# Two branch gates by Strassen's algorithm in a hybrid attention layer, and its forgetting gates in two stages

## The chip, the cores and the metric

One of the eight cores of a Trainium2 chip runs the kernel. The metric is device microseconds of one execution. TensorE multiplies, VectorE (DVE), ScalarE (ACT) and GpSimd (POOL) do the elementwise work, SyncE (SP) issues most loads. The five engines run their own instruction queues in order and wait for each other on semaphores.

## The reference

A layer over 512 frames of 1024 channels, all in float32. With u the normalized input:

```python
proj = u @ w_in          # GLA q,k,v,out-gate g,low-rank alpha | FoX q,k,v,forget | memory query | 3 gates of 1024
y_gla = (rmsnorm(gla(q, k, v, log_a)) * silu(g)) @ w_gla_o      # 4 heads, chunks of 64 frames
y_fox = forgetting_attention(q, k, v, log_f) @ w_fox_o          # 8 heads, causal softmax
y_mem = memory_attention(q, mem) @ w_mem_o                      # 4 heads, 256 memory tokens
merged = sigmoid(gate_gla) * y_gla + sigmoid(gate_fox) * y_fox + sigmoid(gate_mem) * y_mem
h = x + merged @ w_out
h = h + square(relu(rmsnorm(h) @ w_ff1)) @ w_ff2
out = rmsnorm(h)
```

Each of the three gates is a product of 512 x 1024 by 1024 x 1024. A sigmoid is computed as half of 1 + tanh(x/2).

## The kernel before

Every large product runs in three passes. An operand is split into hi, its rounding to the fast float32 format, and lo, the rest; `mm3` (L150 to L153) then adds hi*hi, hi*lo and lo*hi in PSUM. A weight chunk of 128 x 1024 floats (512 KB) is loaded by SP into a ring of three raw buffers; `split_w` makes hi by a cast on ScalarE (L141) and lo by a difference on VectorE (L142), into rings of three hi and three lo tiles. So the split of one chunk can begin when the chunk three earlier has been used up. The activations' hi and lo (`uhi`, `ulo`) stay in SBUF for all projections. `split` (L203, L204) does the same for other operands.

A projected tile (`gT`) is 128 output channels by 512 frames: eight k-steps of `mm3`, 24 matmuls of 512 columns. A generator yields after each `mm3`; one such yield is called a unit here.

The order of TensorE's instructions is that of the program. The other engines' queues are ordered by a planner that simulates when each instruction would be ready. The attention stages are written as lists of steps (scores, transposes, values of one head), and `weave` puts units of other projections between the steps so that TensorE has work while the other engines do the softmax or the decays:

- FoX stage: eight heads, woven with 128 units: GLA keys and queries, the FoX query and key tiles of pairs 2 and 3 (`fox_pair`), GLA values (`gvg`, which takes four PSUM tiles at once) and the four output gates `gla_g`.
- Memory stage: four heads; its own query tiles are steps, and the forgetting branch (`branch("gate_fox", ...)`) is the fill: 96 units.
- GLA stage: `decays`, `key_turn`, `gla_scores`, `states`, `gla_values`, `gla_turn` over two pairs of heads, woven with the memory branch, 96 units.
- Then the GLA branch runs alone, and after it the output projection and the FFN.

A branch does, for each of eight tiles j: the gate tile, tanh on ScalarE (L629), the output tile (12 matmuls), the product (tanh + 1) * y on VectorE (L642, L644); for the second and third branch GpSimd adds it into `acc` (L645). The last branch also splits `acc` for the output projection.

The FFN already uses Strassen's algorithm. Its weight sums are made in DRAM by GpSimd's DMAs, 32 copies and accumulating copies in a fixed order. `next_sum` issues one with every second weight chunk; each waits for that chunk's cast, and for the sum that it builds on.

## Time and profile before

| | |
|---|---|
| median of 3 executions | 845.01 us (844.64 to 846.56) |
| the profiled execution | 845.09 us, span 843.3 us |
| mean granted TensorE clock | 0.995 |
| TensorE busy | 826.6 us (98%) |
| VectorE busy | 557.7 us (66%) |
| ScalarE busy | 438.9 us (52%) |
| GpSimd busy | 92.1 us (11%) |

The profile is of one execution. Busy time of matmuls overlaps, since they are pipelined, so the starts of two instructions give a truer price than the duration of one. In rows of a timeline the first number is the start in us, the second the duration in us, and a bracket holds the idle time of the engine before the instruction and what ended it. In rows of groups, the numbers behind the first bar are the busy time in us and the mean duration in ns, then the engine's idle time just before and its releasers.

### The profile page before, as it was taken

How to read it: one execution, taken by the hardware profiler on the slowest of the kernel's cores; microseconds unless marked ns; L12 is line 12 of the kernel's file. 1: busy time of each engine (PE TensorE's matmuls, PEld its weight loads, DVE VectorE, ACT ScalarE, POOL GpSimd, SP SyncE). 2: the span in 40 equal slices, each digit the busy share in tenths (PEclk: the TensorE clock that was granted, in tenths of full speed). 3: DMA queues.
4: the chain of work that ended last, by engine and by line, in shares of the span. 5: the costliest groups of instructions: out<-in, count | busy, mean ns of one | idle time of the engine just before them, and what ended most of it. 6: DMA issues, size and time to landing. Idle time of an engine off the chain costs nothing.

```text
span 843.3 us, 11909 instructions
## 1 busy us (share of the span) xinstructions
PE 826.6 (98%) x4553; PEld 709.9 (84%) x4553; DVE 557.7 (66%) x899; ACT 438.9 (52%) x695; POOL 92.1 (11%) x114
## 2 busy tenths in 40 slices
PE   8999999999999999999999999999999999999994
PEld 6888888888888888787888889998998899889983
DVE  5856767656444556574543457896689678878896
ACT  6765757654333341321332335875577367637763
POOL 1001000000000021222222100011001100100011
PEclk9999999999999999999999999999999999999998
DMA  8525545354556546257677632978767966895552
GB/s 312 192 100 198 153 151 167 110 174 132 171 147 171 179 137 188 48 174 229 200 181 212 208 123 70 291 173 198 243 196 165 219 218 175 193 256 186 142 97 102
DMA packets 36872, 147.16 MB, mean 174 GB/s; under 512 B 4624, under 2 KB 5584, under 8 KB 34768
## 3 DMA queue, kind: packets, MB, share of 16 engines
q1 hardware_dynamic: 28144, 96.06, 33.0%
q0 software_dynamic: 7168, 46.14, 26.0%
q10 hardware_dynamic: 1504, 4.21, 1.4%
q8 instruction: 35, 0.57, 0.3%
q14 instruction: 21, 0.17, 0.1%
HBM read 144.27 MB, written 31.49 MB: 208 GB/s over the span
## 4 chain that ended last, share of the span: by engine, by line
PE 92%; DVE 4%; DMA 1%; issue 1%; ACT 1%; POOL 0%; SPq 0%; POOLq 0%; DVEq 0%
PE mm L151 25%; PE mm L152 25%; PE mm L153 24%; PE a L152 3%; PE a L151 3%; PE a L153 3%; DVE h L959 1%; DVE lo L204 1%; PE a L794 1%; DMA xn<-in_xN_dram 1%; DMA raw<-in_wst_dram 1%; PE a L516 1%; PE a L811 1%; PE a L517 1%; PE a L549 1%
## 5 line engine op out<-in xcount | busy, mean ns | idle before, releaser
L142 DVE TENSOR_TENSOR wlo<-raw,whi 128x1024 fp32r<-128x1024 f32 x75 | 95.7, 1279 | 80.1 <-ACT whi L141 78.9
L141 ACT CAST whi<-raw 128x1024 fp32r<-128x1024 f32 x75 | 78.8, 1052 | 121.3 <-PE mm L152 96.0
L151 PE MATMUL mm<-uhi,whi 128*128 128x512 f32 x352 | 139.4, 396 | 0.0
L153 PE MATMUL mm<-uhi,wlo 128*128 128x512 f32 x352 | 137.3, 390 | 0.0
L152 PE MATMUL mm<-ulo,whi 128*128 128x512 f32 x352 | 137.2, 390 | 0.0
L203 ACT CAST hi<-raw 128x1024 fp32r<-128x1024 f32 x65 | 68.2, 1049 | 47.5 <-PE mm L152 34.4
L204 DVE TENSOR_TENSOR lo<-raw,hi 128x1024 fp32r<-128x1024 f32 x65 | 79.5, 1223 | 18.6 <-ACT hi L203 18.6
L153 PEld LDWEIGHTS mm<-uhi,wlo 128*128 128x128 f32 x352 | 66.1, 188 | 14.1
L151 PEld LDWEIGHTS mm<-uhi,whi 128*128 128x128 f32 x352 | 66.1, 188 | 13.5 <-issue 0.7
L152 PEld LDWEIGHTS mm<-ulo,whi 128*128 128x128 f32 x352 | 66.2, 188 | 12.7
L152 PE MATMUL mm<-lo,ch 128*128 128x512 f32 x160 | 62.5, 391 | 0.9 <-DVE lo L204 0.9
L152 PE MATMUL mm<-u2l,hi 128*128 128x256 f32 x224 | 63.4, 283 | 0.0
L153 PE MATMUL mm<-u2h,lo 128*128 128x256 f32 x224 | 63.4, 283 | 0.0
L151 PE MATMUL mm<-u2h,hi 128*128 128x256 f32 x224 | 63.4, 283 | 0.0
L203 ACT CAST hi<-b 128x1024 fp32r<-128x1024 f32 x40 | 41.9, 1048 | 40.9 <-PE mm L153 30.4
L153 PE MATMUL mm<-hi,cl 128*128 128x512 f32 x160 | 62.3, 389 | 0.0
L151 PE MATMUL mm<-hi,ch 128*128 128x512 f32 x160 | 62.3, 389 | 0.0
L204 DVE TENSOR_TENSOR lo<-b,hi 128x1024 fp32r<-128x1024 f32 x40 | 48.8, 1223 | 18.2 <-ACT hi L203 18.2
L1143 POOL DMA_DIRECT2D b<-in_wst_dram x32 | 27.6, 863 | 272.2 <-DVE lo L204 209.8
L151 PE MATMUL mm<-u2sh,hi 128*128 128x256 f32 x168 | 47.5, 283 | 0.0
L152 PE MATMUL mm<-u2sl,hi 128*128 128x256 f32 x168 | 47.5, 283 | 0.0
L153 PE MATMUL mm<-u2sh,lo 128*128 128x256 f32 x168 | 47.5, 283 | 0.0
(353 smaller groups left out, 1905.4 us busy)
## 6 DMA issues: line engine op xcount, KB each, us to landing
raw<-in_wst_dram SPq DMA_DIRECT2D x121, 512.0 KB
b<-in_wst_dram POOLq DMA_DIRECT2D x32, 512.0 KB, 5.5
raw<-T SPq DMA_DIRECT2D x28, 512.0 KB
T<-in_wst_dram POOLq DMA_DIRECT2D x12, 1024.0 KB, 8.5
b<-in_wst_dram SPq DMA_DIRECT2D x16, 512.0 KB
T<-in_wst_dram POOLq DMA_DIRECT2D x6, 512.0 KB, 5.3
nFb<-dF ACTq DMA_DIRECT2D x6, 512.0 KB
xn<-in_xN_dram SPq DMA_DIRECT2D x4, 512.0 KB
```

The lines of the kernel that those rows point to most:

```text
L141: cast = nc.scalar.copy(hi, raw)
L142: nc.vector.tensor_tensor(lo, raw, f(hi), op=ALU.subtract)
L151: nc.tensor.matmul(ps, lh, rh, start=start, stop=False)
L152: nc.tensor.matmul(ps, lh, rl, start=False, stop=False)
L153: nc.tensor.matmul(ps, ll, rh, start=False, stop=stop)
L203: nc.scalar.copy(hi, src)
L204: return nc.vector.tensor_tensor(lo, src, f(hi), op=ALU.subtract).ins
L516: nc.tensor.matmul(ps[:, :w], q, K[e][:, 0, :w], start=True, stop=False)
L517: nc.tensor.matmul(ps[:, :w], q, K[e][:, 1, :w], start=False, stop=True)
L549: nc.tensor.matmul(po[:, q0:], vv, PTl[:, c0:c0 + w], start=False, stop=n == 3)
L794: nc.tensor.matmul(ps[:, t, :], kk[:, sl], qq[:, sl], start=True, stop=True)
L1143: nc.gpsimd.dma_start(to[i], wst[index["B", q, i, x]], accum_op=ALU.add)
```

## The change

The gates of the memory and GLA branches are no longer computed tile by tile. Each gate is two groups of four tiles, and a group is one Strassen product of 2 x 2 blocks: weights in blocks 512 channels deep (11, 12, 21, 22; a new kind of chunk, "W"), frames in two halves of 256, seven products of 24 matmuls of 256 columns in place of four tiles of 24 matmuls of 512. All four groups come after the GLA stage (`gate_group`).

- The sums of weight blocks (`plus`) are four GpSimd additions of 128 x 1024 a group. Each is then split like any weight chunk.
- The sums of the activations' blocks are made once: `u_sum` forms two from `uhi` and `ulo` on GpSimd, placed in the GLA stage, and `gate_lefts` forms two more on VectorE and splits all four, in the first group.
- The products are combined on VectorE into `ct` tiles, where the tanh also runs. The output tiles of a group stand between the products.
- The GLA output gates `gla_g` move from the FoX stage to the GLA stage. The forgetting branch is divided: all eight output tiles and the first four gates stay in the memory stage (`fox_out`), the last four gates go to the GLA stage (`fox_late`), with `acc` kept in between.
- So the three attention stages have 96, 64 and 64 units of fill. `weave` takes a weight for each step; the memory stage's steps are in a new order, and the two empty steps of the GLA stage go.
- `next_sum` starts with chunk 19 instead of 9.
- The residual's loads are issued behind the last group, and buffers are shared: raw blocks lie in the tiles of the residual (even groups) or in a tile of the output projection and the `u_sum` tiles (odd groups).

```diff
@@ -45,11 +45,14 @@
     L += [("N", "w_in", 2 * j, OFF["gv"]) for j in range(4)]
     for n, c in (("gg", 4), ("mq", 4)):
         L += [("T", "w_in", OFF[n] + P * j) for j in range(c)]
-    for g, o in (("gate_fox", "w_fox_o"), ("gate_mem", "w_mem_o"), ("gate_gla", "w_gla_o")):
-        for j in range(KT):
-            L.append(("T", "w_in", OFF[g] + P * j))
-            if j % 2 == 0:
-                L.append(("O", o, j // 2))
+    for j in range(KT):
+        L.append(("T", "w_in", OFF["gate_fox"] + P * j))
+        if j % 2 == 0:
+            L.append(("O", "w_fox_o", j // 2))
+    for g, o in (("gate_mem", "w_mem_o"), ("gate_gla", "w_gla_o")):
+        for i in range(2):
+            L += [("W", g, i, b) for b in ("11", "12", "21", "22")]
+            L += [("O", o, 2 * i + 1), ("O", o, 2 * i)]
...
@@ -119,7 +122,7 @@
     def next_sum(after):
         chunk_n[0] += 1
-        op = next(sums, None) if chunk_n[0] > 8 and chunk_n[0] % 2 else None
+        op = next(sums, None) if chunk_n[0] > 18 and chunk_n[0] % 2 else None
-    def weave(steps, units, *gens):
+    def weave(steps, units, *gens, shares=None):
         fill = chain(*gens)
         done = 0
+        shares = shares or [1] * len(steps)
         for i, st in enumerate(steps):
             st()
-            due = units * (i + 1) // len(steps)
+            due = units * sum(shares[:i + 1]) // sum(shares)
             while done < due and next(fill, fill) is not fill:
                 done += 1
         run(fill)
...
-        def gla_g(j):
...
-        steps = []
+        steps, shares = [], []
         for h in range(1, 10):
-            for fn, i in ((fox_values, h - 2), (fox_turn, h - 1), (fox_scores, h)):
+            for fn, i, n in ((fox_values, h - 2, 3), (fox_turn, h - 1, 2), (fox_scores, h, 3)):
                 if 0 <= i < 8:
                     steps.append(partial(fn, i))
-        weave(steps, 128, gla_k(0), gla_k(1), gla_q(0), gla_q(1), fox_pair(2), fox_pair(3), gvg,
-              *[gla_g(j) for j in range(4)])
+                    shares.append(n)
+        weave(steps, 96, gla_k(0), gla_k(1), fox_pair(2), gla_q(0), gla_q(1), fox_pair(3), gvg, shares=shares)
...
-    def branch(gate, wo, oh, ol, n, last=None):
...
+    def o_tile(ow, j, oh, ol, ps):
+        for k in range(4):
+            mm3(ps, ow[0][:, j % 2, k, :], ow[1][:, j % 2, k, :], oh[k], ol[k], k == 0, k == 3)
+            yield
...
+    def fox_gate(j, evac):
+        def tanh(ps):
+            th = mp.tile([P, S], F32, tag="th", name=nm("th"))
+            nc.scalar.activation(th, ps, AF.Tanh, scale=0.5)
+            evac(th)
+        return gT(("T", "w_in", OFF["gate_fox"] + P * j), uhi, ulo, tanh)
+    def fox_out():
         cur = {}
         for j in range(KT):
+            if j < 4:
+                yield from fox_gate(j, lambda th: cur.update(th=th))
             if j % 2 == 0:
+                ow = get_o("w_fox_o", j)
             py = mmt()
+            for i, _ in enumerate(o_tile(ow, j, ofh, ofl, py)):
+                if i == 3:
+                    if j < 4:
+                        nc.vector.scalar_tensor_tensor(acc[j], cur["th"], 1.0, py, op0=ALU.add, op1=ALU.mult)
+                    else:
+                        nc.scalar.copy(acc[j], py)
+                yield
+    def fox_late():
+        for j in range(4, KT):
+            yield from fox_gate(j, lambda th: nc.vector.scalar_tensor_tensor(acc[j], th, 1.0, acc[j], op0=ALU.add, op1=ALU.mult))
...
+        Q, A, T, V_ = (lambda i: run(mem_q(i))), mem_scores, mem_turn, mem_values
+        steps = [(Q, 1), (A, 0), (Q, 2), (T, 0), (A, 1), (V_, 0), (Q, 3), (T, 1), (A, 2), (V_, 1), (T, 2), (A, 3), (V_, 2),
+                 (T, 3), (V_, 3)]
+        weave([partial(*st) for st in steps], 64, fox_out())
     kvst.close()
...
+        def gla_g(j):
...
+        def u_sum(n):
+            x = xsum[n] = xsp.tile([P, 4, 256], F32, tag=f"x{n}", name=f"x{n}")
+            (ah, al), (bh, bl) = (A21, A22) if n == 1 else (A11, A21)
+            nc.gpsimd.tensor_tensor(x, ah, bh, op=ALU.subtract)
+            nc.gpsimd.tensor_tensor(x, x, al, op=ALU.add)
+            nc.gpsimd.tensor_tensor(x, x, bl, op=ALU.subtract)
+        xsum = {}
+        A11, A12, A21, A22 = ([f(t[:, 4 * k:4 * k + 4, 256 * i:256 * i + 256]) for t in (uhi, ulo)] for i in range(2) for k in range(2))
+        steps = (
+            (decays, 0, 10), (key_turn, 0, 3), (gla_scores, 0, 3), (states, 0, 3), (gla_scores, 1, 3), (gla_values, 0, 3),
+            (gla_values, 1, 3), (decays, 1, 3), (gla_turn, 0, 4), (gla_turn, 1, 4), (key_turn, 1, 3), (gla_scores, 2, 3),
+            (states, 1, 3), (u_sum, 1, 0), (gla_scores, 3, 3), (gla_values, 2, 3), (gla_values, 3, 4), (u_sum, 3, 0), (gla_turn, 2, 3),
+            (gla_turn, 3, 3))
+        weave([partial(fn, i) for fn, i, _ in steps], 64, *[gla_g(j) for j in range(4)], fox_late(), shares=[n for *_, n in steps])
...
+        S1, S2, S4 = ([quad(own_tile(i, g)) for g in "hl"] for i in range(3))
+        S3 = [t[:, 0:4, 256:512] for t in (uhi, ulo)]
+        GATE = {1: [t[:, 0:4, 0:256] for t in (uhi, ulo)], 2: [t[:, 4:8, 0:256] for t in (uhi, ulo)],
+                4: [t[:, 4:8, 256:512] for t in (uhi, ulo)], 5: S1, 6: S2, 3: S4, 7: S3}
+        def gate_lefts():
+            split(*S1, xsum[1])
+            for to, (ah, al) in ((S2, A11), (S4, A12)):
+                nc.vector.tensor_tensor(xsum[1], ah, xsum[1], op=ALU.subtract)
+                nc.vector.tensor_tensor(xsum[1], xsum[1], al, op=ALU.add)
+                split(*to, xsum[1])
+            split(*S3, xsum[3])
+        def spare(odd, n):
+            if not odd:
+                return h_tile(n, "wb")
+            return own_tile(3, "hl"[n], F32) if n < 2 else xsp.tile([P, 1024], F32, tag=f"x{2 * n - 3}", name=nm("wb"))
+        def gate_group(gate, wo, oh, ol, i, odd, lefts=None, last=None):
+            raw = {"11": wp.tile([P, 1024], F32, tag="raw", name=nm("raw"))}
+            raw.update({b: spare(odd, n) for b, n in (("12", 0), ("21", 2), ("22", 3))})
+            total = spare(odd, 1)
+            X = [op_.tile([P, 2, S], F32, tag=f"ct{n}", name=nm("ct")) for n in range(2)]
+            (c11, c21), (c12, c22) = ([x[:, :, 256 * n:256 * n + 256] for n in range(2)] for x in X)
+            for b in ("11", "21", "12", "22"):
+                nc.sync.dma_start(raw[b], wst[index["W", gate, i, b]])
+            def plus(to, x, y):
+                nc.gpsimd.tensor_tensor(to, x, y, op=ALU.add)
+            def vec(to, x, y, op=ALU.add):
+                nc.vector.tensor_tensor(to, x, y, op=op)
+            def tanh(x):
+                nc.scalar.activation(x, x, AF.Tanh, scale=0.5)
+            def product(n, src):
+                wh, wl = (t.rearrange("p (a k c) -> p a k c", a=2, k=4) for t in split_w(src))
+                uh, ul = GATE[n]
+                ps = mmt([P, 2, 256])
+                for a in range(2):
+                    for k in range(4):
+                        mm3(ps[:, a, :], wh[:, a, k, :], wl[:, a, k, :], uh[:, k, :], ul[:, k, :], k == 0, k == 3)
+                if n == 1:
+                    nc.scalar.copy(c21, ps)
+                if n == 2:
+                    vec(c11, c21, ps)
+                    tanh(c11)
+                if n == 5:
+                    nc.scalar.copy(c22, ps)
+                if n == 6:
+                    vec(c21, c21, ps, ALU.subtract)
+                    vec(c22, c22, c21, ALU.subtract)
+                if n == 3:
+                    vec(c12, c22, ps)
+                    tanh(c12)
+                if n == 7:
+                    vec(c22, c22, ps, ALU.subtract)
+                    tanh(c22)
+                    vec(c21, c21, ps)
+                if n == 4:
+                    vec(c21, c21, ps)
+                    tanh(c21)
+            ys = {}
+            def output(j):
+                if j % 2 == 0:
+                    ys["w"] = get_o(wo, j)
+                ys[j] = at_()
+                run(o_tile(ys["w"], j, oh, ol, ys[j]))
+            def merge(j):
+                th = X[j % 4 // 2][:, j % 2, :]
+                nc.vector.scalar_tensor_tensor(th, th, 1.0, ys[j], op0=ALU.add, op1=ALU.mult)
+                nc.gpsimd.tensor_tensor(acc[j], acc[j], th, op=ALU.add)
+                if last is not None:
+                    h, l = last
+                    nc.scalar.mul(h[:, j, :], acc[j], 0.5)
+                    nc.vector.scalar_tensor_tensor(l[:, j, :], acc[j], 0.5, f(h[:, j, :]), op0=ALU.mult, op1=ALU.subtract)
+            j = 4 * i
+            product(1, raw["11"])
+            plus(total, raw["11"], raw["12"])
+            product(2, raw["21"])
+            if lefts is not None:
+                lefts()
+            output(j + 2)
+            if lefts is not None:
+                output(j + 3)
+            product(5, total)
+            plus(total, total, raw["22"])
+            if lefts is None:
+                output(j + 3)
+            product(6, total)
+            product(3, raw["22"])
+            plus(raw["12"], raw["12"], raw["22"])
+            plus(total, total, raw["21"])
+            product(7, raw["12"])
+            merge(j + 2)
+            merge(j + 3)
+            product(4, total)
+            output(j)
+            merge(j)
+            output(j + 1)
+            merge(j + 1)
+        gate_group("gate_mem", "w_mem_o", omh, oml, 0, 0, lefts=gate_lefts)
+        gate_group("gate_mem", "w_mem_o", omh, oml, 1, 1)
+        omst.close()
...
+        gate_group("gate_gla", "w_gla_o", ogh, ogl, 0, 0, last=(mh, ml))
...
+        gate_group("gate_gla", "w_gla_o", ogh, ogl, 1, 1, last=(mh, ml))
         for t in range(NT):
             nc.sync.dma_start(hN[t], xN[t * P:(t + 1) * P, :])
-        run(branch("gate_gla", "w_gla_o", ogh, ogl, 2, last=(mh, ml)))
+        nc.sync.dma_start(gf, gffn)
...
+        elif c[0] == "W":
+            _, g, h, (kh, ch) = c
+            ks = slice(512 * (int(kh) - 1), 512 * int(kh))
+            for n in range(2):
+                c0 = OFF[g] + (4 * h + 2 * (int(ch) - 1) + n) * P
+                wst[i, :, 512 * n:512 * n + 512] = W["w_in"][ks, c0:c0 + P].reshape(4, P, P).transpose(1, 0, 2).reshape(P, 512)
```

85 lines of the change are left out of this document (32 added, 53 removed).

## The prediction

> **What bounds the kernel now.** I read the page first (busy shares, chain), then the busy time by stage, because a share over the whole span hides which stage has room.
>
> ```profile
> span 843.3 us, 11909 instructions
> PE 826.6 (98%) x4553; PEld 709.9 (84%) x4553; DVE 557.7 (66%) x899; ACT 438.9 (52%) x695; POOL 92.1 (11%) x114
> PE 92%; DVE 4%; DMA 1%; issue 1%; ACT 1%; POOL 0%; SPq 0%; POOLq 0%; DVEq 0%
> ```
>
> The chain that ended last is TensorE for 92%. The stages, by windows: FoX 78 to 203, memory attention 203 to 308, GLA 308 to 403, GLA gate 403 to 476; the last row is a piece of the FFN.
>
> ```profile
> core 0: us, PE busy (x) PEld busy (x) DVE busy (x) ACT busy (x) POOL busy (x), PEclk, DMA share, GB/s
> 78.00:203.00 125.00, 124.23 (x625) 105.20 (x624) 87.72 (x223) 78.89 (x158) 6.10 (x9) 1.00 0.46 145
> 203.00:308.00 105.00, 105.00 (x502) 88.09 (x502) 48.00 (x80) 38.24 (x75) 5.21 (x8) 1.00 0.55 160
> 308.00:403.00 95.00, 95.00 (x557) 76.59 (x556) 58.23 (x119) 26.20 (x39) 22.62 (x28) 1.00 0.59 170
> 403.00:476.00 73.00, 73.00 (x324) 60.45 (x323) 31.34 (x33) 24.55 (x31) 18.98 (x16) 1.00 0.65 190
> 520.00:560.00 40.00, 40.00 (x284) 37.73 (x283) 35.45 (x41) 28.08 (x41) 3.50 (x4) 1.00 0.82 238
> ```
>
> TensorE sits idle for 0.77 us in the four stages together (125.00 less 124.23). So nothing but TensorE work can be won there, and every wait that the change brings counts in full. The FFN row shows that TensorE can stay unbroken with VectorE at 35.45 of 40 us (89%).
>
> **The Strassen saving.** Busy times of matmuls overlap, so I take starts. In the timeline one gate tile (24 matmuls of 512 columns) runs from the first row to the second; the FFN's products of 256 columns, 18 apart, are the other two.
>
> ```profile
> 411.06 0.39 PE L151 MATMUL mm<-uhi,whi 128*128 128x512 f32 x1
> 416.50 0.39 PE L151 MATMUL mm<-ogh,whi 128*128 128x512 f32 x1
> ...
> 539.80 0.28 PE L151 MATMUL mm<-u2h,hi 128*128 128x256 f32 x1
> 541.96 0.28 PE L151 MATMUL mm<-u2h,hi 128*128 128x256 f32 x1
> ```
>
> (416.50 - 411.06) / 24 = 0.2267 us and (541.96 - 539.80) / 18 = 0.120 us: half the columns cost 53%, not 50%. A group of four gate tiles was 4 x 24 x 0.2267 = 21.76 us; it becomes seven products of 24 x 0.120 = 2.88 us, 20.16 us. Saved: 1.60 us a group, four groups, **6.4 us**. That is 7% of the gates' matmuls where the count of products alone says 12.5%. All other TensorE work moves but stays the same in amount, and so do the bytes of weights (16 chunks of 512 KB for 16).
>
> **FoX stage: GLA output gates leave it.** Fill falls from 128 to 96 units (a unit is three matmuls, 0.68 us). The softmax lead stays wide: head 2's last weights were written at 113.63 and first transposed at 119.89.
>
> ```profile
> 113.14 0.49 DVE L525 TENSOR_SCALAR Pt<-Pt,ri 128x512 f32<-128x512 f32 x1
> ...
> 119.89 0.60 PE L532 MATMUL a<-cst_s,Pt 128*128 128x128 f32 x4
> ```
>
> The two fills between lose 2 x (5.33 - 4.5) x 0.68 = 1.1 us of these 6.3: cost zero, covered by 5 us. The tight place is pair 3. By the weights 3, 2, 3 (sum 61) 42 shares lie before scores of head 6: 96 x 42 / 61 = 66 units, and pair 3's K ends with unit 64, so two units (1.36 us) cover its evacuation. The chain shows how long that took before:
>
> ```profile
> 149.77 0.24 PE mm L153
> 150.13 1.22 DVE wlo L142
> 151.38 0.69 DVE K L204
> 152.10 1.05 ACT K L487
> 153.16 0.59 ACT K L203
> 153.78 0.70 DVE K L204
> 154.62 0.47 PE mm L151
> ```
>
> K's last matmul ended at 150.01 and its first half was complete at 153.15 (ACT K), 3.1 us later; so 3.1 - 1.4 = **+1.8 us** of wait. Bounds: 1.0 (cast, difference and copy alone: 0.59 + 0.70 + 1.05 less 1.36) and 3.1 (the second half's end, 154.48, counted). The 0.77 us that stood here before, when the fourth PSUM tile of v waited for the same evacuation, goes: six units and head 6's scores now lie between. **-0.8 us**.
>
> **Memory stage** (64 units for 96, queries earlier). The shortest lead is transposes to values of head 3: four units, 2.7 us. Before, those transposes ended at 298.6 and the last split at 300.73:
>
> ```profile
> 297.60 1.03 PE L693 MATMUL a<-cst_s,Pm 128*128 128x128 f32 x8
> ...
> 300.05 0.68 DVE L204 TENSOR_TENSOR pl<-a,ph 128x512 fp32r<-128x512 f32 x1
> ```
>
> 2.1 us against 2.7: zero, and 0.7 us if another 1.28 us split gets in between.
>
> **GLA stage** (64 units for 96; output gates and the late FoX gates as fill; two weight-independent sums, three GpSimd operations each, put in).
>
> ```profile
> 308.69 1.05 PE L732 MATMUL a<-cst_s,la 128*128 128x128 f32 x8
> ...
> 316.43 0.69 DVE L748 TENSOR_TENSOR kd<-gkT,ek 128x512 f32<-128x512 f32 x1
> ...
> 319.12 0.60 PE L761 MATMUL a<-cst_s,kd 128*128 128x128 f32 x4
> ```
>
> kd is complete 8.4 us after the decays' first matmul; the new lead is 0.9 + 10 x 0.68 = 7.7 us: **+0.7 us**. The ends are 0 (kd computed before qpos and qneg) and 5 us (the six sums collide with these VectorE products, or the norm's power operation queues behind one at the stage's end). I take 0.7, from the only row that names this wait.
>
> **The gate stage: who prepares the operands.** Groups that carry its prices, and two collisions:
>
> ```profile
> L142 DVE TENSOR_TENSOR wlo<-raw,whi 128x1024 fp32r<-128x1024 f32 x75 | 95.7, 1279 | 80.1 <-ACT whi L141 78.9
> L141 ACT CAST whi<-raw 128x1024 fp32r<-128x1024 f32 x75 | 78.8, 1052 | 121.3 <-PE mm L152 96.0
> ...
> L644 DVE SCALAR_TENSOR_TENSOR th<-th,mm 128x512 f32<-128x512 f32 x16 | 11.0, 686 | 8.4 <-PE mm L153 8.2
> L645 POOL TENSOR_TENSOR acc<-acc,th 128x512 f32<-128x512 f32 x16 | 24.0, 1501 | 63.8 <-DVE th L644 63.8
> ...
> 344.34 1.12 DVE L820 TENSOR_SCALAR on<-a,rr 128x128 f32<-128x128 f32 x4
> 344.50 1.27 POOL L645 TENSOR_TENSOR acc<-acc,th 128x512 f32<-128x512 f32 x1 [0.43 <-DVE th L644]
> ...
> 403.95 1.28 POOL L645 TENSOR_TENSOR acc<-acc,th 128x512 f32<-128x512 f32 x1 [1.89 <-DVE th L644]
> 403.96 2.35 DVE L142 TENSOR_TENSOR wlo<-raw,whi 128x1024 fp32r<-128x1024 f32 x1
> ...
> 436.60 1.23 DVE L142 TENSOR_TENSOR wlo<-raw,whi 128x1024 fp32r<-128x1024 f32 x1
> 436.64 2.33 POOL L645 TENSOR_TENSOR acc<-acc,th 128x512 f32<-128x512 f32 x1 [1.67 <-DVE th L644]
> ```
>
> A VectorE operation with two SBUF operands and a GpSimd add exclude each other: 1.23 becomes 2.35 beside a 1.28 add, and 1.28 becomes 2.33 the other way; the pair took 2.36 us for 2.51, 94%. With a PSUM operand (344.34) neither is slowed. A 128x1024 add is nowhere in the trace; I take twice the 128x512 one, 2.56 us (bounds 1.28 and 2 x 2.33). The Trainium skill, GPSIMD Engine Reference, section Performance versus the Vector engine, gives 4497 ns for a two-input add of 2048 elements and says to use VectorE for elementwise work; by a line through that and the row an estimate of 2.35 us would take 3.4 us off the 16 adds' load below.
>
> TensorE's time for a group is 20.16 + 4 x 12 x 0.2267 = 31.0 us, four groups 124.2. The excluding work of one group: nine weight splits at 1.23, one difference at 0.69, four sums at 2.56, four merges at 1.28: 27.1 us; in the GLA groups four more differences (0.69): 29.9; the first group prepares its left factors with eight more 1.23 operations: 36.9. Together 123.8 us, times 0.94 is **116.4 us beside 124.2**. This load, 94%, is the stage's question. Where it hides is in the three-deep ring of split weights: a split may start when the product three uses earlier ends, which is 5.8 us ahead between products, but 2.88 us for product 3 (the shared output weights before it are held until the second output tile ends). Cast and split take 1.05 + 1.23 = 2.3 us there, so a GpSimd sum at that moment costs up to 2 us. I put the waits at 1.0 us in the first group and 0.3 in each other: **+1.9 us**. Ends: 0 (packing at 94% or better) and 6.6 us (no better than the FFN row's 89%: 116.4 / 0.89 = 130.8); I stay nearer the low end because that row shows no idle TensorE at 89%, so its limit was not reached.
>
> GpSimd's queue also carries the FFN's weight sums, 18 of them here.
>
> ```profile
> T<-in_wst_dram POOLq DMA_DIRECT2D x12, 1024.0 KB, 8.5
> DMA to landing us min/median/max: 3.8/6.2/11.6
> ```
>
> One is due every two of a group's nine chunks: 31.0 / 4.5 = 6.9 us. A sum that needs the one before waits 8.5 - 6.9 = 1.6 us, at worst 4.7, and the adds queue behind it. Second sum (needed for product 6 at 14.1 us into the group, ready to start at 5.2, 4.8 us long with its split): slack 4.1 us. So zero; without that slack 1 to 3 us a time, some four times. SP's loads for a group go to buffers that are free a group ahead; the residual's loads move behind the third group and still have 31 us.
>
> **Sum.** -6.4 - 0.8 + 1.8 + 0.7 + 1.9 = -2.8 us. The profiled execution took 845.09 us (span 843.3; its median of three is 845.01, the same): **842.3 us**.
>
> **Rivals.** (1) *Shared access becomes the bound* (slower). Place: the four groups. The load packs to 88%: 116.4 / 0.88 = 132.3, 8.1 us over TensorE; 845.1 - 7.2 + 2.5 + 8.1 = **848.5**. It decides from 4.7 us of waits, a packing of 90%. For it: the two-way collisions; the first group's load exceeds its 31.0 us. Against: sums can run a group ahead, merges late, and ten VectorE operations a group (6.9 us by L644) read PSUM and can run beside adds. By the skill's rule (GPSIMD Engine Reference, Specifications: SBUF interfaces shared with VectorE, contention for its two-SBUF-input instructions) this rival is what to expect; the trace agrees on the mechanism (2.35 for 1.23), not yet on the price.
> (2) *The thinner fills eat the gain* (no change). Scores of head 6 at 3.1, GLA at 2.5, gate groups 1.9: 845.1 - 7.2 + 7.5 = **845.4**. For it: fills shrink by a quarter to a third. Against: the leads above, of which only two are short.
> (3) *All waits hidden*: 845.1 - 7.2 + 1.0 = **838.9**; against it two places that the order itself makes short.
>
> **How the numbers follow.** A measurement of this kernel can tell 0.2% (1.7 us) from no change. Forecast (839.5 to 843.3) 0.40, rival 3 0.05, rival 2 (843.3 to 846.7) 0.20, rival 1 (846.7 to 855) 0.35. Faster 0.45, same 0.20, slower 0.35. The range takes rival 1 to about its priced middle and a little over: 838.7 to 850.5; that leaves out 0.13 above and 0.03 below. The forecast's own range is 839.5 to 843.3.
>
> **What would show it.** Product starts 0.120 us apart and 24 a product: the saving. An idle TensorE before head 6's first score matmul, released by ACT's K copy, 1 to 3 us: that step; none at 150 to 155. Idle before kd's transposes under 1 us. In the gate stage, waits of TensorE on weight splits or left factors: under 3 us in all for the forecast, 5 to 13 for rival 1, with splits of 2 to 4 us in place of 1.23. Wrong if 128x1024 adds take far from 2.56 us, or if GpSimd stands behind a weight sum's landing for longer than 4 us.

## The result and the profile after

The change makes the kernel slower: 866.97 us (median of 4, 862.84 to 869.8) against 845.49 of the kernel before beside it; ratio 1.025, interval 1.020 to 1.030. Forecast were 842.3 us and a range of 838.7 to 850.5. The profiled execution took 865.02 us.

The page of the changed kernel, the lines that answer to those shown of before (span, busy time, the chain that ended last):

```profile
span 863.2 us, 12589 instructions
PE 830.8 (96%) x4841; PEld 725.4 (84%) x4841; DVE 618.5 (72%) x947; ACT 462.8 (54%) x723; POOL 152.0 (18%) x136
PE 81%; DVE 6%; DMA 5%; issue 2%; POOL 2%; ACT 1%; SPq 0%; POOLq 0%; DVEq 0%; ACTq 0%
```

TensorE's share of the chain falls from 92% to 81%, and DMA has 5%. To place the loss, take starts: where the last attention stage ends, and where the output projection begins (timeline, kernel before, then after):

```profile
402.90 0.39 PE L151 MATMUL mm<-uhi,whi 128*128 128x512 f32 x1
468.18 0.39 PE L151 MATMUL a<-whi,mh 128*128 128x512 f32 x1
```
```profile
343.95 0.28 PE L154 MATMUL mm<-uhi,whi 128*128 128x256 f32 x1
487.87 0.39 PE L154 MATMUL a<-whi,mh 128*128 128x512 f32 x1
```

The output projection begins 19.7 us later; behind it the two take the same. Before, one whole branch ran from 402.90 to 468.18, 65.28 us. After, four groups (two branches) take 143.92 us for 130.56: 13.4 us lost where 6.4 were to be won. The other 6.3 us lie ahead: two branches before 468.18 is 337.62, and the first group begins at 343.95.

By windows, the four groups of after (columns as in the prediction's table):

```profile
343.95:386.17 42.22, 35.24 (x217) 32.42 (x216) 40.50 (x30) 17.90 (x21) 25.60 (x14) 0.92 0.83 265
386.17:418.74 32.57, 31.36 (x218) 29.22 (x216) 23.93 (x20) 12.68 (x15) 18.10 (x12) 1.00 0.85 250
418.74:456.77 38.03, 34.14 (x218) 31.56 (x217) 21.76 (x23) 13.81 (x17) 20.70 (x14) 0.91 0.80 232
456.77:487.87 31.10, 31.10 (x218) 29.16 (x217) 22.05 (x24) 14.34 (x18) 11.10 (x10) 1.00 0.79 219
```

The fourth group is what the arithmetic promised: 31.10 us with TensorE never idle, for 32.64 before (half of 65.28). The first is 11.1 over it, the third 6.9. In the first VectorE is busy 40.50 of 42.22 us. The granted clock falls to 0.92 and 0.91 in just these two. Where TensorE waits, the longest from the FoX stage to the output projection (timeline; in brackets idle time and what ended it):

```profile
159.58 0.58 PE L520 MATMUL a<-K,Q 128*128 128x256 f32 x1 [2.48 <-ACT K L491]
349.09 0.39 PE L154 MATMUL mm<-uhi,whi 128*128 128x256 f32 x1 [2.12 <-ACT whi L144]
367.21 0.39 PE L156 MATMUL mm<-f1h,wlo 128*128 128x256 f32 x1 [3.90 <-DVE wlo L145]
401.89 0.39 PE L156 MATMUL mm<-f1h,wlo 128*128 128x256 f32 x1 [1.21 <-DVE wlo L145]
436.44 0.58 PE L154 MATMUL mm<-f1h,whi 128*128 128x256 f32 x1 [3.42 <-ACT whi L144]
```

These are the scores of head 6 in the FoX stage, products 2 and 6 of group 1, product 6 of group 2 and product 6 of group 3. Shorter ones follow some of them (0.76 at 350.35, 0.21 at 375.09, 0.46 at 437.70).

The wait at product 2 is ScalarE's. Its copy of product 1's result (347.01) stands ahead of the cast of product 2's weights in its queue; the cast begins at 347.99, after 0.39 us more of waiting for the block to land, and takes 1.05.

*Group 1, product 6*: VectorE and GpSimd take turns (timeline, both engines):

```profile
349.96 2.65 POOL L924 TENSOR_TENSOR wb<-raw,wb 128x1024 f32<-128x1024 f32 x1
350.22 3.48 DVE L145 TENSOR_TENSOR wlo<-raw,whi 128x1024 fp32r<-128x1024 f32 x1
352.69 3.27 POOL L924 TENSOR_TENSOR wb<-wb,wb 128x1024 f32<-128x1024 f32 x1
353.62 3.41 DVE L904 TENSOR_TENSOR x<-x,ulo 128x1024 f32<-128x1024 f32 x1
...
362.15 2.80 POOL L924 TENSOR_TENSOR f3l<-raw,f3h 128x1024 f32<-128x1024 f32 x1
362.76 3.27 DVE L904 TENSOR_TENSOR x<-x,ulo 128x1024 f32<-128x1024 f32 x1
365.95 1.21 DVE L145 TENSOR_TENSOR wlo<-wb,whi 128x1024 fp32r<-128x1024 f32 x1
```

The last row is what product 6 waits for; it stands in VectorE's queue behind left factors (x) that took 2.8 to 3.4 us each for 1.23. The sum into f3l is the second group's: the planner drew two of its four into this one.

*Group 2* shows the same drawing ahead: at 393.64 GpSimd begins the first sum of the third group, after standing 4.36 us for that group's block, whose load took 11.83 us from its issue at 381.65. The second group's own sum, for product 6, is behind it in the queue.

*Group 3*: GpSimd stands still (timeline of GpSimd, then two pieces of the chain, start and length):

```profile
413.73 0.81 POOL L129 DMA_DIRECT2D T<-in_wst_dram  x1 [8.00 <-DMA T<-T]
424.38 0.54 POOL L131 DMA_DIRECT2D T<-T  x1 [7.28 <-DMA T<-in_wst_dram]
426.18 2.40 POOL L924 TENSOR_TENSOR f3l<-raw,f3h 128x1024 f32<-128x1024 f32 x1
429.78 2.39 POOL L924 TENSOR_TENSOR f3h<-f3h,wb 128x1024 f32<-128x1024 f32 x1
432.70 2.61 POOL L924 TENSOR_TENSOR wb<-wb,wb 128x1024 f32<-128x1024 f32 x1
```
```profile
405.19 8.03 DMA T<-T
413.73 10.14 DMA T<-in_wst_dram
```

A weight sum of the FFN waits for the one before it to land, twice, 15.3 us in all; the block sums queue behind, two of the fourth group first, and the one for product 6 ends at 435.3. Its cast ends the wait at 436.44.

### The profile page after: what moved, and what is told of

It is laid out like the page before. It is cut to its first block, busy times and chain, and to the rows that moved or that the text cites. A ratio compares the mean times of both kernels' runs of the same rounds, so it can differ in the third digit from the quotient of the medians.

```text
span 863.2 us, 12589 instructions
## 1 busy us (share of the span) xinstructions
PE 830.8 (96%) x4841; PEld 725.4 (84%) x4841; DVE 618.5 (72%) x947; ACT 462.8 (54%) x723; POOL 152.0 (18%) x136
## 3 DMA queue, kind: packets, MB, share of 16 engines
q1 hardware_dynamic: 28144, 96.06, 31.5%
## 4 chain that ended last, share of the span: by engine, by line
PE 81%; DVE 6%; DMA 5%; issue 2%; POOL 2%; ACT 1%; SPq 0%; POOLq 0%; DVEq 0%; ACTq 0%
PE mm L154 20%; PE mm L155 20%; PE mm L156 20%; PE a L155 4%; PE a L154 4%; PE a L156 4%; DVE wlo L145 2%; DMA raw<-in_wst_dram 1%; DMA T<-in_wst_dram 1%; DMA T<-T 1%; PE a L800 1%; DVE x L904 1%; DVE h L1110 1%; DMA xn<-in_xN_dram 1%; PE a L520 1%
## 5 line engine op out<-in xcount | busy, mean ns | idle before, releaser
L154 PE MATMUL mm<-uhi,whi 128*128 128x512 f32 (+1 forms) x352 | 127.0, 361 | 2.1 <-ACT whi L144 2.1
L156 PE MATMUL mm<-uhi,wlo 128*128 128x512 f32 (+1 forms) x352 | 124.6, 354 | 1.0 <-DVE wlo L145 1.0
L155 PE MATMUL mm<-ulo,whi 128*128 128x512 f32 (+1 forms) x352 | 124.3, 353 | 0.0
L145 DVE TENSOR_TENSOR wlo<-raw,whi 128x1024 fp32r<-128x1024 f32 x63 | 81.6, 1298 | 41.4 <-ACT whi L144 41.3
L144 ACT CAST whi<-raw 128x1024 fp32r<-128x1024 f32 x63 | 66.1, 1051 | 72.5 <-PE mm L155 40.6
```

The lines of the kernel that those rows point to most:

```text
L144: cast = nc.scalar.copy(hi, raw)
L145: nc.vector.tensor_tensor(lo, raw, f(hi), op=ALU.subtract)
L154: nc.tensor.matmul(ps, lh, rh, start=start, stop=False)
L155: nc.tensor.matmul(ps, lh, rl, start=False, stop=False)
L156: nc.tensor.matmul(ps, ll, rh, start=False, stop=stop)
```

## The experiments

Times in us; the ratio is to the kernel before on the same chip, with its interval. A group runs from its first product (in f2 from its output tiles) to the next group's. Where the first group is plain (g1, g2), its start is taken 32.64 ahead of the second's.

| kernel | time | ratio | gate stage begins | groups | output projection |
|---|---|---|---|---|---|
| after | 866.97 | 1.025 (1.020 to 1.030) | 343.95 | 42.2, 32.6, 38.0, 31.1 | 487.87 |
| e1_sp | 863.24 | 1.0208 (1.0186 to 1.0229) | 344.75 | 42.2, 31.3, 37.4, 31.1 | 486.77 |
| e2_sums | 862.02 | 1.0187 (1.0170 to 1.0204) | 347.71 | 44.2, 31.1, 31.1, 31.1 | 485.23 |
| e3_dve | 861.03 | 1.0181 (1.0156 to 1.0205) | 342.12 | 45.1, 32.5, 36.1, 31.1 | 486.92 |
| e4_pair | 864.09 | 1.0221 (1.0201 to 1.0242) | 338.82 | 42.6, 37.9, 33.5, 31.1 | 483.82 |
| f1_pair_sums | 853.38 | 1.0091 (1.0074 to 1.0108) | 340.82 | 42.6, 31.1, 31.1, 31.1 | 476.73 |
| f2_first | 856.81 | 1.0135 (1.0120 to 1.0150) | 340.85 | 43.4, 33.5, 31.1, 31.1 | 479.95 |
| f3_nolefts | 860.60, one run | | 343.28 | 39.6, 32.9, 32.6, 31.1 | 479.44 |
| f4_noadd | 849.77, one run | | 342.81 | 36.3, 31.1, 31.5, 31.1 | 472.80 |
| g1_plainfirst | 844.03 | 0.9986 (0.9977 to 0.9996) | 340.6 | 32.6, 31.7, 31.1, 31.1 | 467.13 |
| g2_plain_kd | 842.90 | 0.9971 (0.9961 to 0.9982) | 339.4 | 32.6, 31.7, 31.1, 31.1 | 465.87 |
| g3_order | 858.69 | 1.0161 (1.0145 to 1.0178) | 339.60 | 48.7, 31.1, 31.1, 31.1 | 481.58 |
| f5_lateadds | 852.73 | 1.0085 (1.0068 to 1.0102) | 340.98 | 42.4, 31.1, 31.1, 31.1 | 476.64 |

The first four each take one suspect from the changed kernel.

**e1_sp: the order of SP's queue.** A block of group 2 stands ahead of three blocks of group 1 in SP's queue and waits for a left factor's split (waits of SP's queue, kernel after: total, times, longest):

```profile
SPq L921 <- DVE ulo L208: 25.3, 1, 25.3
```
```diff
+            with ExitStack() as behind:
+                if last_load:
+                    behind.enter_context(tc.issue_after(last_load[0]))
                 for b in ("11", "21", "12", "22"):
-                    nc.sync.dma_start(raw[b], wst[index["W", gate, i, b]])
+                    d = nc.sync.dma_start(raw[b], wst[index["W", gate, i, b]])
+            last_load[:] = [d.ins]
```

> Only the order of SP's queue changes: the weight blocks of a group are issued behind all blocks of the group before. In the changed kernel a block of the second group stood ahead of three blocks of the first and waited 25.3 us for the split of the last left factor. Queue theory: the waits of TensorE for product 2 of the first group (2.12 and 0.76 us) and the half clock behind them (0.58 over 4 us, 1.7 us) go, so the first group takes 37 to 39 us instead of 42.2, the whole 3 to 5 us less. Rival (shared access of VectorE and GpSimd bounds the first group, 36.9 us of excluding work in it): the wait moves to product 6 and the first group still takes 41 to 42 us.

That wait in SP's queue falls to 7.2 us, and ScalarE's cast no longer waits for the block: it starts at 348.30, right behind the copy of product 1's result (347.81). Product 2 still waits 1.62 + 0.90, from ScalarE's order alone, and the clock behind it stays at 1.00 (351 to 355). Yet product 6 then waits 0.87 + 3.93, and group 1 is as long as before. The blocks' late loads do not set its length; the rival's number is met. The whole is 3.7 us lower, less than the 7 us between the executions of the changed kernel.

**e2_sums: the FFN's weight sums earlier**, one with every chunk from the ninth on, so that they are done ahead of the gate stage.

```diff
-        op = next(sums, None) if chunk_n[0] > 18 and chunk_n[0] % 2 else None
+        op = next(sums, None) if chunk_n[0] > 8 else None
```

> The FFN's 32 weight sums are issued with every weight chunk from the 9th on (9th to 40th) instead of every second from the 19th on, so that none is left for the gate stage. Queue theory (GpSimd's additions stand behind sums that wait for the landing of the sum before: 8.0 and 7.3 us of waiting, product 6 of the third group 3.4 us late): second group 31 to 32 us instead of 32.6, third 31 to 32 instead of 38.0; together 6 to 8 us less; the first group stays at 40 to 42. Shared-access theory: the third group keeps at least 3 of its 7 us, since the additions and splits are the same. Price: the attention stages lose under 2 us to the denser transfers.

Groups 2, 3 and 4 take 31.1 us each: their loss of 8.4 us was GpSimd standing behind landings, of weight sums in group 3 and of a block in group 2, which no longer comes late when the sums' transfers are gone. Group 1 takes 44.2, over the expected 40 to 42. And the sums now fall in the FoX stage (windows, kernel e2_sums; the second row is the same window of after):

```profile
78.00:203.00 125.00, 117.42 (x580) 98.31 (x579) 87.23 (x221) 76.01 (x155) 21.03 (x21) 0.99 0.70 205
```
```profile
78.00:203.00 125.00, 121.63 (x602) 102.22 (x602) 85.91 (x220) 78.49 (x158) 19.35 (x11) 0.99 0.35 114
```

The DMA share doubles, TensorE is idle 7.6 us for 3.4, and the gate stage begins 3.8 us later, where under 2 were expected.

**e3_dve: the block sums on VectorE.**

```diff
-                nc.gpsimd.tensor_tensor(to, x, y, op=ALU.add)
+                nc.vector.tensor_tensor(to, x, y, op=ALU.add)
```

> The 16 sums of weight blocks run on VectorE instead of GpSimd, nothing else. Shared-access theory: a 128x1024 sum occupies the shared access for 1.23 us instead of 2.4, and GpSimd no longer stretches splits from 1.23 to 3.4; the wait of 3.9 us at product 6 of the first group shrinks below 1.5 and the whole is 6 us or more faster. Queue theory (what hurts is GpSimd's queue standing behind weight sums, and SP's order): the third group's wait goes too, since no sum of weight blocks is in that queue, but the waits for product 2 stay. A third outcome: VectorE, with 89.6 + 19.7 us of own work in 124, becomes the bound and groups take 33 to 36 us each.

No operation of 3.4 us is left, and VectorE is busy 34.9 us of group 1 instead of 40.5, but the waits only move (1.78 at product 6, 1.65 and 2.49 at product 3) and the group takes 45.1; product 2 waits as before (2.50 and 0.76). The trace shows what makes VectorE's queue late: the two sums of the second group that were drawn into this one now stand in it, ahead of what products 6 and 3 need, and VectorE stood idle 2.60 us before the first of them (360.00) for the second group's block to land. With their own 2 x 1.23 that is 5.1 us, beside 5.9 us of waits at products 6 and 3. So moving the sums to VectorE, in the order that the planner gave it, does not mend group 1; without the drawn sums it was not tried.

**e4_pair: pair 3 ahead of the GLA queries.**

```diff
-        weave(steps, 96, gla_k(0), gla_k(1), fox_pair(2), gla_q(0), gla_q(1), fox_pair(3), gvg, shares=shares)
+        weave(steps, 96, gla_k(0), gla_k(1), fox_pair(2), fox_pair(3), gla_q(0), gla_q(1), gvg, shares=shares)
```

> The query and key tiles of FoX pair 3 come before the GLA query tiles in the fill, 16 units earlier; nothing else. If the short lead of K is the cause, the wait of 2.5 us before the scores of head 6 and the half clock behind it (0.64 over 4 us, 1.4 us) go, and the gate stage begins 3 to 5 us earlier than 343.95. If ACT and VectorE are too busy in the FoX stage whatever the order, another wait of that size comes up at a neighbouring head.

The 2.48 us wait at head 6 goes, and the gate stage begins 5.1 us earlier (0.5 of it already stands at 90 us, ahead of anything that the edit moves). The time gains 2.9. Group 2 now loses 6.8 us: GpSimd stands 6.71 us for the third group's block, and product 6 waits 3.54 (399.21). In the profiled execution TensorE waits 3.63 us more in the output projection (491.69), where GpSimd's last sums into `acc` come behind a weight sum; the profiled executions of e1 and f3 have 1.93 and 2.30 us there, so their whole times say less than their groups.

**f1_pair_sums: both cures**, the sums at a gentler pace.

```diff
-        op = next(sums, None) if chunk_n[0] > 18 and chunk_n[0] % 2 else None
+        op = next(sums, None) if chunk_n[0] > 4 and (chunk_n[0] % 2 or chunk_n[0] > 23) else None
```

> Two repairs together: FoX pair 3 ahead of the GLA queries, and the FFN's weight sums at every second chunk from the 5th to the 23rd (FoX, where dense sums cost 3.8 us in the run before) and at every chunk after that, so that all but a few are done ahead of the gate stage. If the two costs are separate, they add: gate stage begins at 339 to 341 (343.95 before the repairs), groups two to four take 31.1 to 31.5 us, the first 42 to 44, and the whole is 11 to 14 us faster, 852 to 856. If a denser transfer load is what hurts (rival), the attention stages pay 3 us or more and the whole stays above 858.

13.6 us of the 21.5 are back, and what is left of the waits in the gate stage is in group 1: 2.44 and 0.76 at product 2, 3.84 at product 6. Behind the first two the clock is halved (windows, kernel f1_pair_sums; the idle time ends at 346.30):

```profile
343.86:346.30 2.44, 0.00 (x1) 0.01 (x1) 1.82 (x3) 1.69 (x3) 0.00 (x0) 1.00 1.01 400
346.30:348.70 2.40, 1.64 (x11) 1.44 (x12) 2.40 (x2) 0.89 (x1) 2.16 (x2) 1.00 1.03 416
348.70:352.30 3.60, 3.60 (x18) 3.41 (x17) 3.60 (x2) 1.05 (x1) 3.52 (x2) 0.53 0.87 218
352.30:356.00 3.70, 3.70 (x18) 3.01 (x17) 3.70 (x3) 1.05 (x1) 1.40 (x2) 1.00 0.98 235
```

The granted clock is still full for 2.4 us after the first wait (the second lies in that row), then 0.53 for 3.6 us: 3.6 x 0.47 = 1.7 us on top of the waits. The Trainium skill (TensorE: Matmul & The Clock Gate, Part 1: The HAM clock gate) has the clock at half after an idle window of about 3.4 us, in windows that run free. The length of the slow stretch agrees; that waits this short can be enough (here 2.44 and 0.76 us, at head 6 in the kernel after 2.48 alone), the rows show and the rule as stated does not say. Not every such wait brings it: behind the 2.74 us at product 3 of f3 the clock stayed at 1.00 (369 to 376).

**f2_first: a lead for group 1's operands**, by putting its four output tiles ahead of product 1.

```diff
             j = 4 * i
+            if lefts is not None:
+                for n in (2, 3, 0, 1):
+                    output(j + n)
             product(1, raw["11"])
```

> As the run before, and in the first group all four output tiles (10.9 us of TensorE work that needs no left factor) stand ahead of product 1 instead of between and behind the products. Theory of the late start (VectorE can begin the left factors only when the GLA stage's tiles are free, and its load up to product 3 does not fit before it): the first group takes 32 to 36 us instead of 42 to 44, the whole 842 to 848. Theory of the bound (36.9 us of excluding work in the group, however placed): it still takes 38 us or more, since the work only starts 11 us earlier relative to the products but has to finish by the same place.

A lead of 10.9 us, as built, changes nothing: group 1 takes 43.4. Product 2 no longer waits, product 5 waits 2.65 and product 6 4.98 us. But little of the lead reached the other engines. SP still issued the blocks at 340.22, as the order of its queue was not e1's; ScalarE stood 4.36 us for product 2's block (until 348.19), and GpSimd's first sum began at 349.51, 8.7 us into the lead. So the run meets the number of the bound (38 us or more) without deciding for it. From 357.10 on VectorE does one operation after the other (timeline, kernel f2_first):

```profile
357.10 3.37 DVE L145 TENSOR_TENSOR wlo<-wb,whi 128x1024 fp32r<-128x1024 f32 x1
360.40 3.40 DVE L903 TENSOR_TENSOR x<-uhi,x 128x1024 f32<-128x1024 f32 x1
363.83 3.26 DVE L904 TENSOR_TENSOR x<-x,ulo 128x1024 f32<-128x1024 f32 x1
```

**f3_nolefts and f4_noadd** leave work out of the changed kernel: the four VectorE additions of the left factors in f3, the 16 block sums on GpSimd in f4 (products 5, 6, 7 and 4 read plain blocks).

```diff
-                nc.vector.tensor_tensor(xsum[1], ah, xsum[1], op=ALU.subtract)
-                nc.vector.tensor_tensor(xsum[1], xsum[1], al, op=ALU.add)
```
```diff
-            plus(total, raw["11"], raw["12"])
-            product(5, total)
-            plus(total, total, raw["22"])
-            product(6, total)
+            product(5, raw["12"])
+            product(6, raw["12"])
```

> The changed kernel with the four VectorE additions that form the left factors of products 6 and 3 left out (the splits stay): 4.9 us less VectorE work in the first group. If VectorE's chain of left factors sets product 6, its wait (3.9 us) goes and the first group takes 36 to 38 us, with only the wait at product 2 left; if GpSimd's additions set it, the wait stays within 1 us.

> The changed kernel with the 16 GpSimd sums of weight blocks left out (products 5, 6, 7 and 4 read a plain block). Shared-access theory: splits and left-factor additions in the first group take 1.23 us each instead of up to 3.4, the wait at product 6 goes, the group takes 36 to 38 us; the third group's wait goes too, for want of an addition to wait for. Rival (VectorE's own chain and the order of its queue): the first group stays above 40.

Without the left factors' additions product 6's wait goes, but product 3 waits 2.74: 2.6 us are won in group 1, which takes 39.6 where 36 to 38 were expected. Without the block sums every wait in group 1 but product 2's goes (2.47 and 0.75, with the slow clock behind them): 36.3 us, so 5.2 of the 11.1 us stand without any GpSimd sum. VectorE's load of the group (windows, kernel f4_noadd; 30 operations, as in the row of after):

```profile
342.81:379.12 36.31, 33.09 (x218) 30.76 (x217) 28.49 (x30) 17.73 (x21) 8.02 (x8) 0.95 0.95 317
```

28.49 us against 40.50 for as many operations: GpSimd's six sums in that group, 14.4 us at 2.40, cost VectorE 12.0.

**g1_plainfirst: the first group without Strassen**, on top of f1: four gate tiles of 512 columns as in the kernel before, with the left factors made beside them.

```diff
-        gate_group("gate_mem", "w_mem_o", omh, oml, 0, 0, lefts=gate_lefts)
+        plain_group(OFF["gate_mem"], "w_mem_o", omh, oml)
```

> As f1 (the fourth pair of FoX heads ahead of the GLA queries, the weight sums paced from the fifth chunk on), and the first of the four groups is computed as before the change: four gate tiles of 24 matmuls of 512 columns, four output tiles, four merges, with no block additions; the left factors of the other three groups are made meanwhile. Theory A (VectorE and GpSimd cannot prepare four left factors and the operands of seven products in the first 31 us; any order of them shows the wait): with the left factors beside a group that asks only for casts, the first group takes 32.6 us (65.3 for two groups in the kernel before), the other three 31.1 each, the output projection starts at 340.8 + 32.6 + 93.3 = 466.7 against 476.7 in f1, and the time is 853.4 - 10.0 = 843.4 (842.5 to 845.5), 1 to 3 us under the kernel before. Theory B (the first Strassen group waits wherever it stands, because its own adds and casts begin cold): groups 32.6, then about 38, then 31.1 twice: 850. Theory C (the left factors and the subtractions of the last S3 are late for the second group, which waits once, 2 to 3 us, and pays the clock): 846 to 848.

Theory A's number was 843.4, measured 844.03; the output projection was to start at 466.7 and starts at 467.13. The left factors and the block sums fit when they are not in one group, and product 2's wait is gone too.

**g2_plain_kd: and more fill behind head 0's decays.**

```diff
-            (decays, 0, 10), (key_turn, 0, 3), (gla_scores, 0, 3), (states, 0, 3), (gla_scores, 1, 3), (gla_values, 0, 3),
+            (decays, 0, 13), (key_turn, 0, 3), (gla_scores, 0, 2), (states, 0, 2), (gla_scores, 1, 2), (gla_values, 0, 3),
```

> As g1, and of the 64 steps of gate projections that fill the GLA stage more stand behind the decays of head 0 (share 13 instead of 10, taken from the scores of heads 0 and 1 and the states of head 0). The theory that the GLA stage waits 0.7 us for the decayed keys of head 0 because its filler ends too early: the gap goes, time 0.7 below g1's. Rival: the filler that is taken away is then missing behind one of the three thinned steps, where a wait of 0.3 to 1 us opens: same as g1 or up to 0.5 slower.

The 0.71 us wait for kd goes and no other opens; the time is 1.1 us lower (0.7 was expected). This version is faster than the kernel before by 0.29% (interval 0.18 to 0.39). Windows of its gate stage (kernel g2_plain_kd; the first begins 0.4 us ahead of the plain group, the second is the second group):

```profile
339.00:372.02 33.02, 33.02 (x147) 27.33 (x146) 24.21 (x20) 13.21 (x17) 7.98 (x4) 1.00 0.62 220
372.02:403.67 31.65, 31.35 (x218) 29.21 (x216) 20.55 (x20) 12.73 (x15) 20.78 (x10) 1.00 0.28 100
```

VectorE needs 24.2 and 20.6 us where it needed 40.5 and 23.9 in the first two groups of after.

**g3_order: product 2's cast and difference ahead of the left factors** (f1, with e1's order of loads).

```diff
-                lefts()
+                with tc.issue_after(cast_now[0]), tc.issue_after(sub_now[0]):
+                    lefts()
```

> As f1, with the cast and the subtraction of product 2's weights ahead of the left factors on ScalarE and VectorE in the first group, and a group's block loads behind those of the group before. Theory A (product 2's wait of 2.44 + 0.76 us is only the place in the two queues, while the 3.84 us at product 6 are the sum of VectorE's and GpSimd's work): product 2 no longer waits, and what was ahead of it is late for product 5, 6 or 3 by as much, since the left factors begin 2 us later: the first group stays within 1.5 us of 42.6 and the time within 1.5 us of 853.4. Rival B (two independent waits): product 2's two waits and the slow clock behind them go, 3.2 + 1.7 = 4.9 us, 848.5.

Product 2 no longer waits. An output tile then waits 5.64 and product 3 5.01 + 1.41, and group 1 takes 48.7. Neither number was met: theory A had the direction, the size was missed by 5 us. Two splits show why (timeline, kernel g3_order):

```profile
342.57 3.53 DVE L208 TENSOR_TENSOR f0l<-x,f0h 128x1024 fp32r<-128x1024 f32 x1
346.02 3.36 DVE L208 TENSOR_TENSOR ulo<-x,uhi 128x1024 fp32r<-128x1024 f32 x1
```

In f1 these two stand ahead of GpSimd's first sum and take 1.23 and 1.22, the second before the group begins. Here both fall beside the first two sums, and from 341.43 to 373.56 VectorE stands idle for only 1.11 us.

**f5_lateadds: the next group's sums behind the last sum of the group before** (f1).

```diff
+                    if last_add and to is total:
+                        behind.enter_context(tc.issue_after(last_add[0]))
```

> As f1, but a group's first two block sums (on GpSimd) issue behind the last sum of the group before. In f1 GpSimd makes the second group's first sum at 358.81 (3.34 us), in the first group, and VectorE's x at 360.46 takes 2.78 us beside it for 1.23, ahead of the weight difference on which product 6 waits 3.84 us. Theory (each addition that is drawn into the first group costs VectorE its own length): that x takes 1.23, product 6's wait shrinks by 1.5 to 2.3, and the first group by as much or a little more, 42.6 to 39.5 - 41; the second group stays at 31.1 with both sums behind product 6 of the first; time 850 to 852 against 853.4. Rival A: the second group then lacks its first sum and waits 1 to 3 us at product 5: 853 to 855. Rival B (the wait at product 6 is set by the group's own second sum and left factors alone): no change in the wait, 853.4.

As expected the left factor takes 1.21 again and product 6's wait falls from 3.84 to 1.57. The group stays at 42.4: products 3, 7 and 4 now wait 1.41, 0.19 and 0.82, because the group's own last sum and the two that follow stand beside their differences (timeline, kernel f5_lateadds):

```profile
366.69 3.37 POOL L929 TENSOR_TENSOR f3l<-raw,f3h 128x1024 f32<-128x1024 f32 x1
370.14 3.27 POOL L929 TENSOR_TENSOR f3h<-f3h,wb 128x1024 f32<-128x1024 f32 x1
```

So both drawn sums are later but still inside group 1, which ends at 383.35, and VectorE is busy 40.3 us in it as in f1 (40.5). The expected 850 to 852 is missed a little (852.73), and what group 1 takes without the drawn sums was not measured. The order of the work was moved three ways (f2, g3, f5) and no order took group 1 below 42.2 us; less work did (f3, f4, g1). None of the three is a clean test of order: f2's lead was eaten by late blocks, g3 pushed two splits beside sums, and f5 kept the load.

## Why the prediction was wrong

Step by step:

- **The Strassen saving, 1.60 us a group**: right. An undisturbed group takes 31.10 for 32.64, 1.54 less.
- **Scores of head 6, +1.8**: the wait was found by the right rows and was 2.48, inside 1.0 to 3.1. Its price was not: with that pair earlier the stage ends 5.1 us sooner. The term counted idle time alone; the granted clock behind the wait was 0.64 for 4 us (160 to 164), which is 1.4 us, and e4 took away a wait of 0.57 too. With the 0.5 us that e4's execution had at 90 us already, about 0.2 of the 5.1 is not accounted for.
- **The wait for v's tile, -0.8; the memory stage, 0; kd, +0.7**: right. No wait of v's, none of the memory stage is in the trace of after, and kd's is 0.71, which g2 closes. The six sums of activations cost nothing.
- **Length of a GpSimd sum, 2.56**: 2.40 when undisturbed. The estimate by the Trainium skill (GPSIMD Engine Reference, Performance versus the Vector engine), 2.35, was nearer.
- **Operand preparation, +1.9**: the step that failed first. Its own count gave the first group 36.9 us of excluding work against TensorE's 31.0, and then spread it over the stage (116.4 of 124.2). But a group's left factors are needed in that group, and what is free in group 4 is no use to group 1. With the two sums drawn in from group 2 it is 36.9 + 2 x 2.56 = 42.0, at the rows' 94% 39.5, and VectorE was busy 40.5 of 42.2. That the two are so near is partly luck: the first holds GpSimd's four merges (5.1 us), the second VectorE's ten operations on PSUM (6.9 us by the prediction's count). What it cost, measured: 11.1 us, of it 6.99 of waits and 4.1 beyond them, 3.4 of these by the granted clock (0.92 over 42.2 us). 5.9 of the 11.1 go with the block sums (f4). The other 5.2 are, in f4, product 2's wait and the clock behind it, for which the prediction had no term: it let a split begin when its place in the ring is free, and the cast stood behind a copy in ScalarE's queue. g3 took that wait away and lost more elsewhere; with a plain first group (g1) both are gone. The bound of 6.6 us came from the same mean over the stage. Rival 1 had the mechanism but the same pooling, hence its 848.5; the sign given for it was met (12.1 us of waits in the gate stage, splits of 3.4 us).
- **GpSimd behind the weight sums, 0**: the second failure, 6.9 us (group 3, gone in e2 and f1). The prediction spaced the sums 6.9 us apart, so that GpSimd would stand only for what a landing takes beyond that: 1.6 us by the median of 8.5, at worst 4.7 by the longest, 11.6, against a slack of 4.1. The landings were no longer than that (8.03 and 10.14 us); the spacing was not there. GpSimd came to each waiting sum soon after it had issued the one before, and stood 8.00 and 7.28 us, 15.3 in all. The prediction named this as what would make it wrong (a stand of over 4 us) but gave it no chance. f3 kept these sums and its third group took 32.6, so how much of the stand reaches TensorE depends on when it falls.
- **SP's loads, 0**: a block did wait 25.3 us, against "free a group ahead"; e1 shows that it cost little in group 1, and in f2 it spoiled the lead. The third group's first block was issued well ahead (381.65), but the planner drew its sum into the second group, GpSimd stood for it, and that group lost 1.5 us. In f1 the block was issued at 378.85, and the same sum, at 382.98, did not wait for it.
- **The clock**: no step had it. In groups 1 and 3 the length beyond 31.10 and the waits (6.99 and 3.88 us) is 4.1 and 3.0 us.

The sum by measured terms, to 19.7 us of later output projection: 6.3 ahead of the gate stage (5.1 of it by e4), 11.1 in group 1, 8.4 in groups 2 and 3, less 4 x 1.54 = 6.2 saved, which leaves 0.1 to rounding. f1 takes away 11.1 of it and g1 9.6 more.

What stays open: whether another order of the same work, with no sum drawn in from the next group, e1's loads and product 2's cast ahead of the copy, could bring group 1 near its load; no run has all three.

## What to carry to other kernels

Hold the load of a helper engine against the stretch in which its results are needed, not against the whole stage: a sum of 94% can hide a first group at 119%. Where an engine both computes and issues transfers that wait for each other, the second wait counts from the first one's landing, and everything behind it in the queue is late by both. When a planner orders the queues, look for work of the next piece that it drew ahead of work due now: if its operand has not landed, the engine stands for it. Price a wait of TensorE above some 2 us with the slow clock that can follow, and when a saving is the same for each piece but the preparation falls on the first, try the first piece the old way.

## What the runs showed of the hardware

- Two-way exclusion at this size: beside back-to-back GpSimd sums of 2.40 us a VectorE operation with two SBUF operands takes 2.8 to 3.5 us for 1.23, and the sum up to 3.4. The Trainium skill (SBUF — State Buffer, SBUF: two separate sides) describes an exclusive lock held for the whole instruction; the rows agree.
- Waits of TensorE of 2.48 us (head 6 in after, 0.50 from 160 to 162) and of 2.44 and 0.76 us (product 2 in f1) were followed by a stretch of about half the granted clock, in f1 2.4 us later and 3.6 us long. Behind the single wait of 1.21 us in group 2 of after the clock stayed at 1.00 (windows 401 to 403 and 403 to 407), and so it did behind 2.74 us in f3 (369 to 376): the length of a wait alone did not decide it.
